# When a unit's weight blocks are split and where a side computation stands: four edits to a two-layer transformer kernel

## The chip, the cores and the metric

The kernel runs as one program on one core of a Trainium2 chip. The metric is device time in microseconds from start to end of the program. TensorE does the matmuls, VectorE (DVE) and ScalarE (ACT) the elementwise work, GpSimd (POOL) some more of it, SyncE (SP) issues most of the DMAs. Each engine runs its instructions in the order in which the program lists them.

## The reference

Two layers, each of them FFN half, mixer, FFN half, over 512 sample tokens and 128 prompt tokens (640 together) of width 1024. Every sub-layer normalises, scales and shifts its input by numbers from the condition, and adds its gated output:

```python
mod = (jax.nn.silu(cond) @ mod_w[l] + mod_b[l]).reshape(cond.shape[0], 3 * N_SUB, D_MODEL)

def adaln_sublayer(x, mod, s, g_pre, g_post, fn, weight):
    shift = mod[:, 3 * s, None]
    scale = mod[:, 3 * s + 1, None]
    gate = mod[:, 3 * s + 2, None]
    h = rmsnorm(x, g_pre) * (1 + scale) + shift
    y, aux = fn(h)
    return x + weight * gate * rmsnorm(y, g_post), aux

def swiglu(h, w_in, w_out):
    gate, up = jnp.split(h @ w_in, 2, axis=-1)
    return (jax.nn.silu(gate) * up) @ w_out
```

`w_in` is 1024 x 5632, `w_out` 2816 x 1024, and each layer has two of each. The condition has two rows (sample and prompt), so that each of the nine modulation rows of a layer is a product of a 2 x 1024 matrix with a 1024 x 1024 piece of `mod_w`. The four FFN halves hold most of the time; the change is in them.

## The kernel before

**Split products.** Every float32 factor is split in two: ScalarE casts it to the high part (`whi`, L171), VectorE subtracts that from it (`wlo`, L172), and TensorE adds three products: high with high, high with low, low with high. The weights are loaded by SP (L103) into three buffers `raw` of 512 KB, and `Stream` splits them in the order in which they are used, with at most five split blocks held.

**Parts and units.** An FFN half takes its 22 columns of 128 hidden features in six parts of 2, 4, 4, 4, 4, 4. Part 0 is done in the plain way. In parts 1 to 5 each column of 128 is a `Unit`: gate and up are one product of two by two blocks, done with seven products of blocks rather than eight. A product is 12 matmuls of 320 tokens (L717). The weight side is four blocks, X, S, Z and V. X is the gate as loaded. Four operations of GpSimd (L157, `_combine`) then make the others out of gate and up: S in a buffer of its own (`part_tile`), Z and V in the place of what was loaded. The token side is four sums of blocks of `hT`, made once per FFN half by `combine()` (L689, L692, on VectorE and GpSimd) and split into `b20` to `b41`.

**The order of a unit.** `strassen` (L790) writes it out: p2, p3 of the unit ahead, p6, p5, p7, p1 of the unit behind, p4. The products p1, p6, p7 and p4 add into one bank: between two of them ScalarE copies the bank to SBUF (L736 after p1, L747 after p6, L760 after p7), so that p7 can't begin before the copy L747 is done. Only p5 stands between. p2 ends with a subtraction on VectorE (L741) and a SiLU on ScalarE (L742), p3 with L774 on VectorE, a SiLU (L775) and a multiplication (L776); then the result is split (L379, L380) into `g`. The numbers behind the products in `strassen` say how many blocks of the next unit are split there: two after p2, one after p6, one after p4. In a part's last unit none is; there `Stream.pump` splits the blocks of `w_out` as places come free.

**Behind the units** of a part stand the products with `w_out` (L825): ten banks of 512 columns, 12 matmuls each in a part of four, evacuated by L848 or L850. In part 5 they are the tail (`emit`), with the post-norm, gate, residual and the next pre-norm.

**The side computation.** `Modulation` makes rows for later sub-layers, half a row (512 columns) at a time. `on_v` does it on VectorE: 16 operations (L438, L440), two for each of eight 128-row blocks, and then four small matmuls (L452) which sum over the partitions. `on_t` does it on TensorE with 32 matmuls (L472) in two steps. Both share three buffers `mod` of 512 KB with the accumulator. `stage` hands out the work: one half row by `on_v` beside the `w_out` products of each of parts 0 to 4, in 11 steps over that stretch (7 places in part 0, 15 in the others), the rest by `on_t` in the units of parts 1 to 4. When a stage begins, what is left of the last is issued at once. Of the 32 half rows 17 are on VectorE and 15 on TensorE.

**The last part** begins with `load_gate` (L510 to L522: the norm's weights and the two gate rows are loaded, L515 and L519, and multiplied on VectorE, L520) and `load_pre` (scale and shift for the next sub-layer, L504, with two small operations on VectorE, L507).

`in_order` pins the order of the instructions of each engine from part 0 to the end of the units.

## Time and profile before

| | |
|---|---|
| median of 2 runs | 2886.86 us (2885.67 to 2888.05) |
| the profiled execution: its own time | 2889.99 us |
| its span, first to last instruction | 2888.2 us |
| TensorE busy in it | 2595.2 us, 90% |
| mean granted TensorE clock | 0.953 |

The profile's page gives the busy time of each engine and the granted clock of TensorE in 40 slices. The waits of an engine, the order in time, and busy time and clock in chosen stretches are answers of the trace. "gap" or the number in square brackets is the idle time of the engine just before an instruction, and behind the arrow stands what ended it.

### The profile page before, as it was taken

What the parts mean: (1) busy time and instruction counts of PE and PEld (TensorE: products, weight loads), DVE (VectorE), ACT (ScalarE), POOL (GpSimd) and SP (SyncE); (2) the same over time, 40 slices, a digit from 0 to 9 for tenths busy, and PEclk for the clock granted to TensorE, in tenths of its full rate; (3) what the DMA queues carried; (4) which work ended last, traced back from release to release, by engine and by line L of the source; (5) the groups of instructions that cost most, each with busy time, mean ns of one, the idle gap of its engine ahead of it and who ended that gap; (6) DMA issues with size and microseconds to landing.
All of it is one profiled execution on the core that took longest, in us unless ns stands there. A gap on an engine that the chain in (4) does not pass through costs nothing.

```text
span 2888.2 us, 40550 instructions
## 1 busy us (share of the span) xinstructions
PE 2595.2 (90%) x15930; PEld 2295.2 (79%) x15930; DVE 1796.6 (62%) x2847; ACT 1163.5 (40%) x2179; POOL 666.4 (23%) x612
## 2 busy tenths in 40 slices
PE   7788998999989979999887899988999997999988
PEld 5677887888866868888776788877899887888877
DVE  5754566576576576665666656666777766654545
ACT  3323232464455533333253233324655653333323
POOL 1212241210010122222222222213433202222212
PEclk9899999999999989999998999999999998999999
DMA  7344454321201234443343434443222242322133
GB/s 237 96 136 126 134 174 127 117 65 52 70 25 52 97 103 119 120 127 97 82 167 88 131 120 133 119 98 117 76 64 70 63 133 61 103 74 81 52 95 110
DMA packets 356696, 296.95 MB, mean 103 GB/s; under 512 B 44364, under 2 KB 289048, under 8 KB 356504
## 3 DMA queue, kind: packets, MB, share of 16 engines
q1 hardware_dynamic: 352040, 281.25, 32.7%
q10 hardware_dynamic: 2880, 9.18, 0.8%
q0 software_dynamic: 1584, 3.93, 0.5%
q8 instruction: 125, 2.05, 0.3%
q14 instruction: 67, 0.55, 0.1%
HBM read 282.24 MB, written 15.97 MB: 103 GB/s over the span
## 4 chain that ended last, share of the span: by engine, by line
PE 41%; DVE 14%; ACT 5%; DMA 4%; issue 3%; POOL 1%; SPq 1%; ACTq 0%; DVEq 0%; POOLq 0%
PE ps L717 14%; PE ps L825 12%; DVE wlo L172 6%; PE ps L634 4%; PE ps L624 4%; ACT whi L171 4%; PE ps L1072 3%; DMA raw<-in_ffn_w_out_dram 2%; DVE mod L440 1%; PE ps L2019 1%; PE ps L2000 1%; DVE xn L689 1%; PE ps L569 1%; POOL tok L548 1%; DMA mod<-in_mod_w_dram 1%
## 5 line engine op out<-in xcount | busy, mean ns | idle before, releaser
L172 DVE TENSOR_TENSOR wlo<-raw,whi 128x1024 fp32r<-128x1024 f32 x400 | 482.8, 1225 | 245.6 <-ACT whi L171 237.5
L717 PE MATMUL ps<-hT,whi 128*128 128x320 f32 x2560 | 580.4, 314 | 0.0
L825 PE MATMUL ps<-whi,g 128*128 128x512 f32 x1760 | 572.5, 402 | 2.3 <-DVE g L380 1.1
L717 PE MATMUL ps<-b,whi 128*128 128x320 f32 x1920 | 461.1, 328 | 110.5 <-ACT tok L747 76.6
L157 POOL TENSOR_TENSOR raw<-raw 128x512 f32<-128x512 f32 x160 | 208.8, 1305 | 1410.7 <-DVE wlo L172 1157.0
L171 ACT CAST whi<-raw 128x1024 fp32r<-128x1024 f32 x400 | 409.5, 1045 | 268.8 <-PE ps L825 198.6
L717 PEld LDWEIGHTS ps<-hT,whi 128*128 128x128 f32 x2560 | 432.9, 191 | 16.0 <-issue 10.8
L717 PEld LDWEIGHTS ps<-b,whi 128*128 128x128 f32 x1920 | 344.6, 202 | 125.8 <-ACT tok L747 84.2
L717 PE MATMUL ps<-hT,wlo 128*128 128x320 f32 x1280 | 405.1, 317 | 20.3 <-DVE wlo L172 20.3
L825 PEld LDWEIGHTS ps<-whi,g 128*128 128x128 f32 x1760 | 341.1, 194 | 81.6 <-DVE g L380 3.0
L825 PE MATMUL ps<-wlo,g 128*128 128x512 f32 x880 | 353.8, 402 | 0.0
L717 PE MATMUL ps<-b,wlo 128*128 128x320 f32 x960 | 311.3, 324 | 0.0
L634 PE MATMUL ps<-hT,whi 128*128 128x384 f32 (+1 forms) x1216 | 277.9, 316 | 0.0
L717 PEld LDWEIGHTS ps<-hT,wlo 128*128 128x128 f32 x1280 | 243.6, 190 | 32.0 <-DVE wlo L172 29.7
L634 PEld LDWEIGHTS ps<-hT,whi 128*128 128x128 f32 x1216 | 204.1, 189 | 21.9 <-issue 15.2
L825 PEld LDWEIGHTS ps<-wlo,g 128*128 128x128 f32 x880 | 170.6, 194 | 37.4
L717 PEld LDWEIGHTS ps<-b,wlo 128*128 128x128 f32 x960 | 194.1, 202 | 0.0
L634 PE MATMUL ps<-hT,wlo 128*128 128x384 f32 (+1 forms) x608 | 188.8, 311 | 0.0
L440 DVE SCALAR_TENSOR_TENSOR mod<-mod,cc 128x512 f32<-128x512 f32 x238 | 183.6, 824 | 1.2 <-DMA mod<-in_mod_w_dram 1.2
L624 PE MATMUL ps<-hT,whi 128*128 128x384 f32 (+1 forms) x640 | 140.7, 311 | 1.6 <-DVE hT L380 1.6
L634 PEld LDWEIGHTS ps<-hT,wlo 128*128 128x128 f32 x608 | 114.6, 188 | 1.1 <-issue 0.8
L624 PEld LDWEIGHTS ps<-hT,whi 128*128 128x128 f32 x640 | 107.5, 190 | 2.9 <-DVE hT L380 2.5
(407 smaller groups left out, 3705.0 us busy)
## 6 DMA issues: line engine op xcount, KB each, us to landing
raw<-in_ffn_w_in_dram SPq DMA_DIRECT2D x172, 512.0 KB
mod<-in_mod_w_dram SPq DMA_DIRECT2D x128, 512.0 KB
raw<-in_ffn_w_out_dram SPq DMA_DIRECT2D x88, 512.0 KB
raw<-in_na_w_qkv_dram SPq DMA_DIRECT2D x24, 512.0 KB
raw<-in_ab_w_in_dram SPq DMA_DIRECT2D x22, 512.0 KB
raw<-in_mod_w_dram SPq DMA_DIRECT2D x32, 256.0 KB
xs<-x ACTq DMA_DIRECT2D x15, 512.0 KB
b<-xs SPq DMA_DIRECT2D x15, 512.0 KB
```

Source lines behind the costliest of these rows:

```text
L157: self.nc.gpsimd.tensor_tensor(out=out, in0=in0, in1=in1, op=op)
L171: self.nc.scalar.copy(hi[:, :k * n], raw[:, :k * n])
L172: self.nc.vector.tensor_tensor(out=lo[:, :k * n], in0=raw[:, :k * n], in1=hi[:, :k * n].bitcast(F32), op=ALU.subtract)
L440: nc.vector.scalar_tensor_tensor(out=acc[:, c], in0=raw[:, k % 2], scalar=w, in1=acc[:, c], op0=ALU.mult, op1=ALU.add)
L548: eng.tensor_tensor(out=yg[:, c0:c0 + n], in0=src, in1=G[cond_of(t)][:, c0:c0 + n], op=ALU.mult)
L569: nc.tensor.transpose(ps[k // 4][:, k % 4, :], xn[:, k * 128:(k + 1) * 128], ident)
L624: nc.tensor.matmul(out=banks[grp], lhsT=w[a][:, k, :], rhs=hT[b][:, k, o:o + n], start=(k == 0 and (a, b) == (0, 0)), stop=(k == NK - 1 an ...
L634: nc.tensor.matmul(out=banks[grp], lhsT=w[a][:, k, :], rhs=hT[b][:, k, o:o + n], start=(k == 0 and (a, b) == (0, 0)), stop=(k == NK - 1 an ...
L689: eng.tensor_tensor(out=H[key], in0=B[key][0].bitcast(F32), in1=B[key][1].bitcast(F32), op=ALU.add)
L717: nc.tensor.matmul(out=out, lhsT=w[a][:, k, :], rhs=b[c][:, k, :], start=start and (k, a, c) == (0, 0, 0), stop=(k == 3 and (a, c) == PASS ...
L825: nc.tensor.matmul(out=out, lhsT=g[a][kf][:, t * 128:(t + 1) * 128], rhs=w[b], start=(kf == 0 and (a, b) == (0, 0)), stop=(kf == len(fts) ...
L1072: nc.tensor.matmul(out=y[t][h], lhsT=hT[a][:, k, t * 128:(t + 1) * 128], rhs=ws[k // 2, h][b][:, k % 2, :], start=(k == 0 and (a, b) == (0 ...
```

## The change

1. **Splits.** One block after each of p2, p7, p1 and p4 of a unit that isn't the last of its part, rather than two after p2 and one each after p6 and p4; the unit's first p2 takes part too. What p2 does on ScalarE (SiLU) is issued after the block's split. What p3 does on ScalarE, and the multiplication, waits until p6 of the next unit has issued its copy (`rest` in `Unit.later`).
2. **Modulation.** None in part 0. One half row on VectorE in each of parts 1 to 4, one step after each p5 and five beside the `w_out` products; its loads are 256 KB each, in two buffers `mraw`, the accumulator is `macc`. Half rows on TensorE are spread evenly over parts 1 to 4, with the buffers `G1` and `traw`. Now 14 half rows are on VectorE and 18 on TensorE.
3. **S** lies in two halves of one buffer, `G0`, or `macc` in the last part, rather than in `G0` and `G1` by turns.
4. **Gates.** In the last part the norm's weights and the two gate rows are loaded one by one after p7 of its first three units, and multiplied where the scheduler finds a place.

`qkn` moved from one pool to another, and the scratch `junk` to another buffer.

```diff
 class Modulation:
+        def __init__(self, pool, todo, n_v):
+            units = [(l, r, h) for l, r in todo for h in range(D // self.N)]
+            n_t = max(len(units) - n_v, 0)
+            self.loads = {
+                "v": [(*u, k, 1) for u in units[n_t:] for k in range(NK)],
+                "t": [(*u, k, 2) for u in units[:n_t] for k in range(0, NK, 2)],
+            }
...
+        def load(self, kind):
+            while self.loads[kind] and len(self.raws[kind]) < 2:
+                l, r, h, k, n = self.loads[kind].pop(0)
+                if kind == "v":
+                    raw = self.pool.tile([128, 1, self.N], F32, tag="mraw", name="mraw", bufs=2)
+                elif next(self.turn) % 2:
+                    raw = self.pool.tile([128, 2, self.N], F32, tag="traw", name="traw", bufs=1)
+                else:
+                    raw = state.tile([128, 2, self.N], F32, tag="G1", name="G1")
+                nc.sync.dma_start(out=raw, in_=kblock(I["mod_w"][l], k, n, r * D + h * self.N, self.N))
...
+        def start(self, places):
+
+            self.load("v")
+            self.load("t")
+            self.rate, self.owed = 3 * self.n_t / places, 0.0
+
+        def tick(self, v=False):
+            if v:
+                next(self.v, None)
             self.owed += self.rate
             while self.owed >= 1.0:
                 self.owed -= 1.0
-                next(self.it, None)
+                next(self.t, None)
...
-    def load_gate(l, s, weight):
+    def gate_steps(l, s, weight):
 
         gp = big("tok", [128, D])
         nc.sync.dma_start(out=gp, in_=I["norm_post"][l, s].partition_broadcast(128))
+        yield
         out = []
         for c in range(2):
             g = state.tile([128, D], F32, tag=f"G{c}", name=f"G{c}")
             nc.sync.dma_start(out=g, in_=modrows[l][3 * s + 2][c].partition_broadcast(128))
+            out.append(g)
+            yield
+        for g in out:
             nc.vector.scalar_tensor_tensor(out=g, in0=g, scalar=weight, in1=gp, op0=ALU.mult, op1=ALU.mult)
-            out.append(g)
-        return out
+        yield out
...
             def p2(self):
                 W, t = bank([128, HALF]), self.t
                 self.product(W, self.half(self.X, 1), B[1, 0], True)
                 nc.vector.tensor_tensor(out=t[:, 0], in0=t[:, 0], in1=W, op=ALU.add)
-                nc.scalar.activation(out=t[:, 0], in_=t[:, 0], func=AF.Silu)
                 self.done("X")
+                return lambda: nc.scalar.activation(out=t[:, 0], in_=t[:, 0], func=AF.Silu)
...
                 nc.vector.tensor_tensor(out=t[:, 1], in0=t[:, 1], in1=self.Z, op=ALU.add)
-                nc.scalar.activation(out=t[:, 1], in_=t[:, 1], func=AF.Silu)
-                nc.vector.tensor_tensor(out=t[:, 1], in0=t[:, 1], in1=t[:, 2], op=ALU.mult)
+
+                def rest():
+                    nc.scalar.activation(out=t[:, 1], in_=t[:, 1], func=AF.Silu)
+                    nc.vector.tensor_tensor(out=t[:, 1], in0=t[:, 1], in1=t[:, 2], op=ALU.mult)
+                    self.out(1 if self.last else 0, 2)
...
-                todo = [(u.p1, ())] if begin else []
-                todo.append((u.p2, () if begin else (item, item)))
+                todo = [(u.p1, 0)] if begin else []
+                todo.append((u.p2, 1))
                 if not begin:
-                    todo.append((us[i - 1].p3, ()))
-                todo += [(u.p6, () if end else (item,)), (u.p5, ()), (u.p7, ())]
-                todo.append((fill if end else us[i + 1].p1, ()))
-                todo.append((u.p4, () if end else (item,)))
+                    todo.append((us[i - 1].p3, 0))
+                todo += [(u.p6, 0), (u.p5, 0), (u.p7, 1), (fill if end else us[i + 1].p1, 1), (u.p4, 1)]
...
+                    after = fn()
...
+                    for _ in range(0 if end else n):
+                        item()
+                    if after:
+                        after()
                     stream.pump()
+                    if fn == u.p7 and gates and not end:
+                        next(gates)
+                    tick(fn == u.p5)
...
-                mod.stage("t", len(mod.units), 1)
-                mod.stage("t", 0, 1)
-                stream.part_tile = lambda: fp.tile([128, 512], F32, tag="mod", name="mod", bufs=3)
-                G = load_gate(l, s, 0.5)
+                mod.finish()
+                stream.part_tile = part_tiles(lambda: fp.tile([128, 2, 512], F32, tag="macc", name="macc", bufs=1))
+                gates = gate_steps(l, s, 0.5)
...
-                if not last:
-                    mod.stage("t", n_t[p], 7 * len(fts))
-                strassen(fts, g, fill)
+                if p == 1:
+                    mod.start(sum(11 * n - 1 for n in PARTS[1:-1]))
+                strassen(fts, g, fill, gates if last else None)
...
-                mod.stage("v", 1, 4 * len(fts) - 1)
-                for _ in outs:
+                for n, _ in enumerate(outs):
                     stream.pump()
-                    tick()
+                    tick(p > 0 and n in (2, 4, 6, 8, 12))
```

ScalarE in the first FFN half, part 1, from the third unit's p4 to the last unit's p7. `whi` is the high part of a block, `ps` a bank, `tok` and `xn` hold a unit's three products. Before (`raw_1073`, `raw_1217` are the last unit's gate and up, `raw_1223` and `raw_1388` the first two blocks of `w_out`):

```order
L171 CAST whi_1365<-G1_1285 128x512
L742 ACTIVATE tok_1337<-tok_1337 128x320
L171 CAST whi_1384<-raw_1217 128x1024
L171 CAST whi_1390<-raw_1073 128x1024
L171 CAST whi_1396<-raw_1223 128x1024
L775 ACTIVATE xn_1166<-xn_1166 128x320
L171 CAST whi_1422<-raw_1388 128x1024
L747 COPY tok_1337<-ps_1338 128x320
L379 CAST g0_2_905<-xn_1166 128x640
L171 CAST whi_1443<-raw_1394 128x1024
L760 COPY tok_1337<-ps_1338 128x320
```

Now (`raw_1005`, `raw_1141` are the last unit's gate and up, `raw_1160` and `raw_1289` the first two blocks of `w_out`):

```order
L171 CAST whi_1266<-G0_1025 128x512
L759 COPY tok_1270<-ps_1271 128x320
L171 CAST whi_1285<-raw_1141 128x1024
L171 CAST whi_1304<-raw_1005 128x1024
L171 CAST whi_1324<-raw_1160 128x1024
L766 ACTIVATE tok_1270<-tok_1270 128x320
L171 CAST whi_1349<-raw_1289 128x1024
L770 COPY tok_1270<-ps_1271 128x320
L800 ACTIVATE xn_1122<-xn_1122 128x320
L387 CAST g0_2_861<-xn_1122 128x640
L171 CAST whi_1372<-raw_1308 128x1024
L783 COPY tok_1270<-ps_1271 128x320
```

The SiLU of p3 (L775, now L800) went from ahead of the copy after p6 (L747, now L770) to behind it. The cast of the second block of `w_out` stands ahead of that copy in both; the last unit's Z and V, whose splits free the buffers into which that block and the one after it are loaded, went from behind p2 to behind p1 and p4.

VectorE in the first FFN half at the end of part 0, where the token side's blocks are made and split. Before:

```order
L172 TENSOR_TENSOR wlo_846<-raw_684,whi_845 128x1024
L692 TENSOR_TENSOR xn_749<-xn_749,tok_747 128x1280
L440 SCALAR_TENSOR_TENSOR mod_770<-mod_804,cc_93,mod_770 128x512 x2
L380 TENSOR_TENSOR b21_717<-xn_749,b20_716 128x1280
L440 SCALAR_TENSOR_TENSOR mod_770<-mod_804,cc_93,mod_770 128x512 x2
L380 TENSOR_TENSOR b31_719<-xn_748,b30_718 128x1280
L692 TENSOR_TENSOR tok_750<-tok_750,xn_749 128x1280
L380 TENSOR_TENSOR b41_721<-tok_750,b40_720 128x1280
L455 TENSOR_TENSOR mrow_765<-ps_891,mrow_765 128x256
L741 TENSOR_TENSOR xn_911<-xn_911,ps_926 128x320
```

Now:

```order
L172 TENSOR_TENSOR wlo_818<-raw_684,whi_817 128x1024
L715 TENSOR_TENSOR xn_745<-xn_745,tok_743 128x1280
L388 TENSOR_TENSOR b21_717<-xn_745,b20_716 128x1280
L388 TENSOR_TENSOR b31_719<-xn_744,b30_718 128x1280
L715 TENSOR_TENSOR tok_746<-tok_746,xn_745 128x1280
L388 TENSOR_TENSOR b41_721<-tok_746,b40_720 128x1280
L764 TENSOR_TENSOR xn_875<-xn_875,ps_890 128x320
L172 TENSOR_TENSOR wlo_905<-raw_696,whi_904 128x1024
L455 TENSOR_SCALAR macc_939<-mraw_867,cc_93 128x512 x2
L784 TENSOR_TENSOR xn_875<-xn_875,ps_926 128x320
```

The half row's 16 operations are gone from between the token side's, and the first step of one now stands in the first unit of part 1.

VectorE in the first FFN half at the start of the last part, up to the second unit's p7. `mcol` holds scale and shift for the next sub-layer. Before:

```order
L850 TENSOR_TENSOR x4_715<-x4_715,ps_4100 128x512
L455 TENSOR_TENSOR mrow_3981<-ps_4141,mrow_3981 128x256
L520 SCALAR_TENSOR_TENSOR G0_4153<-G0_4153,tok_4151 128x1024
L520 SCALAR_TENSOR_TENSOR G1_4156<-G1_4156,tok_4151 128x1024
L507 SCALAR_TENSOR_TENSOR mcol_4159<-mcol_4159,gcol_4160 128x8 x2
L741 TENSOR_TENSOR xn_4168<-xn_4168,ps_4183 128x320
```

Now (`...` stands for the rest of the first unit):

```order
L878 TENSOR_TENSOR x4_715<-x4_715,ps_4135 128x512
L527 SCALAR_TENSOR_TENSOR mcol_4186<-mcol_4186,gcol_4187 128x8 x2
L764 TENSOR_TENSOR xn_4195<-xn_4195,ps_4210 128x320
...
L764 TENSOR_TENSOR tok_4280<-tok_4280,ps_4320 128x320
L172 TENSOR_TENSOR wlo_4335<-raw_4152,whi_4334 128x1024
L797 TENSOR_TENSOR xn_4195<-xn_4195,ps_4247 128x320
L801 TENSOR_TENSOR xn_4195<-xn_4195 128x320
L388 TENSOR_TENSOR g1_0_4182<-xn_4195,g0_0_4178 128x640
L544 SCALAR_TENSOR_TENSOR G0_4404<-G0_4404,tok_4278 128x1024
```

The gate rows' multiplications (L520, now L544) stood ahead of the first unit's L741; now the first of them stands in the second unit, behind its p6. The two operations on `mcol` stay where they were.

## Rows read from the trace of the kernel before

**Rows 1.** The page: busy time of the engines, and TensorE's granted clock in 40 slices of the span.

```profile
PE 2595.2 (90%) x15930; PEld 2295.2 (79%) x15930; DVE 1796.6 (62%) x2847; ACT 1163.5 (40%) x2179; POOL 666.4 (23%) x612
...
PEclk9899999999999989999998999999999998999999
```

**Rows 2.** The waits of TensorE: what waited for what, microseconds in total, how many times, the longest.

```profile
PE ps L717 <- ACT tok L747: 76.6, 29, 4.2
PE ps L452 <- DVE mod L440: 63.0, 4, 16.1
PE ps L717 <- ACT xn L747: 33.9, 13, 8.8
PE ps L472 <- DMA mod<-in_mod_w_dram: 27.5, 10, 7.0
PE ps L717 <- DVE wlo L172: 20.3, 36, 0.7
```

**Rows 3.** The order in time, TensorE: the product p7 that waits for L747 in the last unit of a part, the first and the last of 20; then the same in the first unit of an FFN half's last part, the first and the last of 4. Columns: start, microseconds, engine, line, operation, names, shapes, count, and in brackets the idle time before and what ended it.

```profile
171.50 0.90 PE L717 MATMUL ps<-b,whi 128*128 128x320 f32 x2 [3.88 <-ACT tok L747]
...
2844.87 0.90 PE L717 MATMUL ps<-b,whi 128*128 128x320 f32 x2 [3.46 <-ACT tok L747]
...
506.85 0.90 PE L717 MATMUL ps<-b,whi 128*128 128x320 f32 x2 [7.40 <-ACT xn L747]
...
2798.13 0.90 PE L717 MATMUL ps<-b,whi 128*128 128x320 f32 x2 [5.62 <-ACT xn L747]
```

**Rows 4.** The order in time around one of the 20, in the second FFN half, engine by engine: TensorE, ScalarE, SyncE.

```profile
1092.48 0.64 PE L717 MATMUL ps<-b,whi 128*128 128x320 f32 x2 [4.00 <-ACT tok L747]
...
1091.06 1.04 ACT L171 CAST whi<-raw 128x1024 fp32r<-128x1024 f32 x1 [1.00 <-DMA raw<-in_ffn_w_out_dram]
1092.01 0.42 ACT L747 COPY tok<-ps 128x320 f32<-128x320 f32 x1
...
1086.72 2.63 SPq L103 DMA_DIRECT2D raw<-in_ffn_w_out_dram  x3
```

**Rows 5.** The chain of work that ended last, in order of time: two products L717 of a unit, back to back, and the products L825 behind them.

```profile
1098.13 3.52 PE ps L717 x24
1101.65 25.78 PE ps L825 x111
```

**Rows 6.** Stretches of time: length, busy time of PE, PEld, DVE, ACT, POOL with counts, granted clock, DMA share, GB/s. The first is behind the wait of rows 4, the second the bubble at the end of a part 0, the third behind a wait at the start of a last part.

```profile
1092.40:1098.10 5.70, 5.62 (x22) 5.18 (x23) 3.41 (x4) 2.13 (x4) 0.00 (x0) 0.70 0.65 209
1021.60:1037.60 16.00, 0.00 (x0) 0.00 (x0) 16.00 (x18) 6.11 (x8) 0.00 (x0) 0.59 0.58 164
1407.20:1414.00 6.80, 6.79 (x37) 6.80 (x38) 1.71 (x2) 2.27 (x4) 4.49 (x4) 0.77 0.01 2
```

**Rows 7.** The order in time at the end of part 0 of the second FFN half: TensorE's next work, and p7 of the first unit; VectorE's first sum of the token side and its last split; GpSimd's two sums.

```profile
1037.65 1.64 PE L452 MATMUL ps<-mod,ones 128*32 128x256 f32 x8 [16.08 <-DVE mod L440]
...
1047.43 0.46 PE L717 MATMUL ps<-b,whi 128*128 128x320 f32 x2
...
1009.79 4.24 DVE L689 TENSOR_TENSOR xn<-hT,hT 128x1280 f32<-128x1280 f32 x1
1018.05 1.48 DVE L689 TENSOR_TENSOR xn<-hT,hT 128x1280 f32<-128x1280 f32 x1
...
1042.30 1.49 DVE L380 TENSOR_TENSOR b<-tok,b 128x1280 fp32r<-128x1280 f32 x1 [1.33 <-ACT b L379]
...
1009.15 7.70 POOL L689 TENSOR_TENSOR tok<-hT,hT 128x1280 f32<-128x1280 f32 x2
```

**Rows 8.** The same stretch, busy time of the lines L440 and L438 alone: length, busy time of DVE with count, granted clock, DMA share, GB/s.

```profile
1009.70:1043.80 34.10, 9.66 (x14) 0.75 0.27 77
1009.70:1043.80 34.10, 3.57 (x2) 0.75 0.27 77
```

**Rows 9.** The order in time at the start of the same FFN half's last part: TensorE's p1 and p7 of the first unit, SyncE, VectorE.

```profile
1393.33 0.56 PE L717 MATMUL ps<-hT,whi 128*128 128x320 f32 x2
...
1407.20 0.90 PE L717 MATMUL ps<-b,whi 128*128 128x320 f32 x2 [6.58 <-ACT xn L747]
...
1395.67 0.36 SPq L515 DMA_DIRECT2D tok<-in_norm_post_dram  x1
...
1397.50 4.92 SPq L504 DMA_DIRECT2D mcol<-mod  x2
...
1405.77 0.17 DVE L507 SCALAR_TENSOR_TENSOR mcol<-mcol,gcol 128x8 f32<-128x8 f32 x1 [1.26 <-DMA mcol<-mod]
```

**Rows 10.** The order in time, TensorE: one modulation step that doesn't wait.

```profile
1068.61 1.08 PE L472 MATMUL ps<-mod,cc 128*32 128x128 f32 x32
```

**Rows 11.** Groups of instructions by line and shape: busy time, mean ns of one, idle time before.

```profile
L172 DVE TENSOR_TENSOR wlo<-raw,whi 128x1024 fp32r<-128x1024 f32 x400 | 482.8, 1225 | 245.6 <-ACT whi L171 237.5 <-issue 1.2 <-PE ps L1295 0.7
...
L157 POOL TENSOR_TENSOR raw<-raw 128x512 f32<-128x512 f32 x160 | 208.8, 1305 | 1410.7 <-DVE wlo L172 1157.0 <-DMA mrow<-in_mod_b_dram 69.3 <-DMA raw<-in_ffn_w_in_dram 42.1
```

**Rows 12.** The order in time, VectorE: two modulation operations and a split of S with GpSimd idle, then the same beside GpSimd's operations.

```profile
1390.41 1.40 DVE L440 SCALAR_TENSOR_TENSOR mod<-mod,cc 128x512 f32<-128x512 f32 x2
...
1379.06 0.68 DVE L172 TENSOR_TENSOR wlo<-G,whi 128x512 fp32r<-128x512 f32 x1
...
1376.20 2.94 DVE L440 SCALAR_TENSOR_TENSOR mod<-mod,cc 128x512 f32<-128x512 f32 x2
...
1081.79 1.80 DVE L172 TENSOR_TENSOR wlo<-G,whi 128x512 fp32r<-128x512 f32 x1
```

More of the change, by code (lines that the diff above doesn't have):

```diff
@@ L421, in bias @@
+        def bias(self, l, r, h, n, parts):
+            tag = f"mrow{n}"
+            row = self.pool.tile([128, n], F32, tag=tag, name=tag, bufs=1)
+            c0 = r * D + h * self.N
             for p, o in parts:
@@ L467, in on_t @@
                 for i in range(2):
-                    raw = self.raws.pop(0)
+                    raw = self.raws["t"].pop(0)
                     for k2 in range(2):
@@ L475, in on_t @@
                             )
-                self.load()
+                self.load("t")
+                if q == 0:
+                    row = self.bias(l, r, h, n, parts)
                 yield
```

122 lines of the change are left out of this document (54 added, 68 removed).

## The prediction

> **What bounds the kernel now.** I read the page first: TensorE is busy for 90% of the span, at a mean clock of 0.953 [rows 1]. So about 290 us are idle, and more is lost to the lower clock; nothing but TensorE's own waits is worth a look. Next its waits [rows 2]. Five of them make 221 us, and all lie in the four FFN halves, in places that the change touches. Then the order in time at each place:
>
> *Ends of parts.* In each part's last unit p7 waits for the copy L747, 20 times, at most 4.2 us [rows 2, 3]. Added up one by one they are 73 of the 76.6 us on `tok`, 3.7 us each. ScalarE is held by the cast of a `w_out` block that is still under way: its load was issued at 1086.72, as soon as the last unit's Z was split, and p7 began at 1092.48, 5.8 us later [rows 4].
>
> *Ends of part 0.* Four waits of 16 us for the modulation's accumulator [rows 2, 7]. VectorE does the half row between the operations that make the token side.
>
> *Starts of last parts.* Four waits of 5.6 to 8.8 us [rows 2, 3], with 28 of the 33.9 us on `xn`. VectorE stands at the gate rows' and `mcol`'s loads, p2's subtraction behind them [rows 9].
>
> *Modulation on TensorE* waits 27.5 us for its loads, and there are 29 us of short waits: 20.3 for `wlo`, the rest for L747 [rows 2].
>
> Behind a long wait the granted clock is 0.70 over 5.7 us, and 0.77 over 6.8 us [rows 6]: parts at 1.2 GHz instead of 2.4. TensorE had stood idle just before. That costs 0.30 x 5.7 = 1.7 us and 0.23 x 6.8 = 1.6 us more. At full clock a product takes 3.52 / 2 = 1.76 us [rows 5], a unit of seven 12.3 us.
>
> **The change, part by part.** *Splits.* The last unit's Z is now split behind its p1, with p4, p2, p3, p6 and p5 before p7: 5 x 1.76 = 8.8 us. Cast 1.05 and subtraction 1.23 [rows 4, 11] and the copy of p1 ahead of them (0.42 as L747) end 2.7 us after p1, and the 5.8 us from the load's issue to p7 are then over at 8.5 us. So the wait would just go. But where a modulation step now stands beside the unit, VectorE is later. GpSimd's four operations, 1.3 us each [rows 11], run in the same stretch, and beside them two modulation operations took 2.94 us, not 1.40, and a split of S 1.80, not 0.68 [rows 12]. I count 1.5 us of lateness, with 0 and 4 us (the wait of today) as the bounds, in the 14 parts that have such a step, and 0.3 in the other 6. That leaves 23 of 73 us: **50 us gained**. Of the slow clock, 20 x 1.7 = 34 us, I take two thirds: **23**.
>
> The short waits for `wlo` and L747 should nearly all go. Z is split three products earlier, and p3's SiLU no longer stands ahead of the copy that p7 needs. I leave 5 of 29: **24**.
>
> Taking the splits forward asks for the loads sooner. From the end of p1 to p6 of the next unit, which needs S, stand ten products, 17.6 us. Z's split (up to 4.6 us with the lateness above), two GpSimd operations (2.6), S's cast (half a block's, 0.6 as estimated from 1.04 for a whole one) and its split (1.8) take 9.6, so a load may take 8 us before TensorE feels it. One took 4.3 in the rows: the cast of 1091.06 waited for it from 1086.72 [rows 4]. What remains is load traffic of the modulation beside it; I charge **10 us** for new waits in the units, bounds 0 and 60.
>
> *Part 0.* VectorE loses 9.66 + 3.57 = 13.2 us of modulation in that stretch [rows 8]. Its last split ended at 1042.30 + 1.49 = 1043.8, so now at 1030.6. On the other side the second sum L689 (1.48 us alone) moves up beside GpSimd's 7.70 us and will take 4.2 as the first does [rows 7]: 1033.3. Then p2's subtraction, SiLU and the copy follow, 0.5 each by the copy's row [rows 4], and p7 begins at about 1034.9 instead of 1047.43. That is 12.5 us four times, slow clock included: **50**. TensorE still stands some 6 us there, since p1 could start at 1021.6 and p7 at 1028.6.
>
> *Last part.* The gate loads leave SyncE's queue ahead of `mcol`'s: 1395.67 to 1397.50 [rows 9]. The last half row on VectorE ends three of 15 places sooner, which is 24 of 120 matmuls of 25.78 / 111 = 0.23 us [rows 5], or 5.5 us, so that SyncE is past its store earlier too. Both bring `mcol`'s last operation, 1405.77, to about 1398.7, before p7 is due at 1393.3 + 4 x 1.76 = 1400.4 less the 1.5 us of subtraction, SiLU and copy. The multiplications now stand behind p6 of the second and third unit, and there VectorE may wait a little for a gate row; S and Z of the next unit have over 3 us in hand. I leave 3 of 28: **25**, and **6** for the clock. On SyncE the two gate rows are now queued ahead of `w_out` loads; at 0.4 us an issue that is hidden as long as those have the 8 us above.
>
> *Modulation on TensorE.* Even spacing over 172 places puts a step with its two loads at every seventh place or later, and a unit of 12.3 us has seven; three loads issued within 2.63 us began to land after 4.3 [rows 4], so two should be there in time. I leave 2 of 27.5: **25**, and **5** for the clock, bounds 0 and 10. Three more half rows cost 6 steps of 1.1 to 1.3 us [rows 10], 7 us; three groups L452 fewer give back 2: **minus 5**.
>
> *VectorE in all.* 48 operations fewer but more of them beside GpSimd. With a modulation step a unit asks VectorE for three splits of 1.23, one of 1.8, the two operations of 2.9, and some 3.3 us of small ones, 11.7 us of a unit's 12.3. That fits, with little to spare. About this the Trainium skill ("SBUF — State Buffer", section "SBUF: two separate sides") says that VectorE with two SBUF inputs and GpSimd take one shared port pair as an exclusive lock, the loser waiting for a whole instruction. By that rule the 2.94 us would be usual, and GpSimd late as well. The trace agrees as far as 2.94 against 1.40 goes [rows 12].
>
> **Sum.** 50 + 23 + 24 - 10 + 50 + 25 + 6 + 25 + 5 - 5 = 193 us. The profiled execution's own time is 2889.99, 3 us above the median of 2886.86: 2890 - 193 = 2697, and against the median 2694. I predict **2695 us**, 6.7% less.
>
> **Rivals.** *All of it goes.* The waits are 221 us and the clock behind them about 34 + 6 + 8; less the 5 us of added work and part 0's unavoidable 24 that is 240: 2650 us. For it speaks that the 8.5 us just fit into 8.8. Chance 0.2.
>
> *VectorE becomes the bound in the units.* 56 units carry a modulation step. If operations beside GpSimd cost as in rows 12 and GpSimd is held up in turn, each unit is 1 us longer, 56 us, and the ends of parts keep two thirds of their wait, 25 us more, with the clock 10: 2785 us. Against it speaks the 11.7 of 12.3. By the skill's rule this is the way it goes; the rule counts in this chance, 0.2.
>
> *SyncE's one queue makes it slower.* Its order now mixes weight loads with 256 KB loads that wait for VectorE and 512 KB loads that wait for TensorE. A weight load behind one of them is as late as it is. It decides once a load needs over 8 us from its place in the queue to landing. To lose 2% it would take 193 + 58 = 251 us, or 4.2 us in each of the 60 units that aren't a part's first (4 x 5 x 3), so a load of 12 us. Rows 4 have three issues in 2.63 us and nothing near that: 2945 us, chance 0.05.
>
> *It does not do what it says:* p7's copy is held by the `w_out` cast as before, since the load is still issued too late, and part 0 is held by its own sums. Then only the modulation's waits and the last part's gain stays, some 60 us: 2830 us, chance 0.07.
>
> **Chances and range.** The forecast, 2660 to 2740, has 0.48. The range should take in the first two rivals: 2640 to 2790. A measurement of this kernel can tell about 2% from no change. Faster by over 2% means under 2829: 0.48 + 0.2 + 0.2 and half of the last rival, 0.91. Slower 0.05, the same 0.04.
>
> **What would show it.** Right: the waits of p7 for the copy behind p6 fall from 110 us to under 40; none of 16 us behind part 0, with 5 to 8 us instead; none above 2 us at the start of a last part; L472 waits for next to nothing; the granted clock is above 0.97. Wrong: new waits of p5, p6 or p7 for `wlo` or a SiLU in units with a modulation step (VectorE), casts on ScalarE that wait for weights loaded by SyncE in the middle of a part (the queue), or a bubble behind part 0 as long as before.

## The result and the profile after

The changed kernel takes **2651.26 us** (median of 2 runs, 2650.78 to 2651.73) against 2886.86: ratio 0.918, 95% interval 0.914 to 0.922. That is 236 us less, where the forecast's sum was 193 us and its range reached from 2640 to 2790.

From the page after, for [rows 1]:

```profile
PE 2528.0 (95%) x16098; PEld 2250.9 (85%) x16098; DVE 1821.9 (69%) x2797; ACT 1170.8 (44%) x2179; POOL 718.0 (27%) x612
...
PEclk9899999999999999999999999999999999999999
```

TensorE does 168 matmuls more and is busy 67 us less; the difference to the span, its idle time, fell from 293 to 121 us. So 172 us of the gain are waits and 67 are matmuls that run sooner at the higher clock (mean 0.984 instead of 0.953). TensorE's waits after, in the places of [rows 2], in microseconds, times and the longest:

```profile
PE ps L740 <- ACT xn L759: 34.1, 4, 8.9
...
PE ps L740 <- ACT tok L770: 8.6, 10, 1.6
...
PE ps L740 <- ACT xn L770: 2.7, 3, 1.4
PE ps L740 <- DVE tok L784: 2.4, 8, 0.6
...
PE ps L740 <- ACT tok L783: 1.2, 2, 0.6
```

L740 is the product (before L717), L770 the copy behind p6 (before L747), L759 the copy of p1. No wait for `wlo`, for modulation loads or for the modulation's accumulator is left. The new wait is that of p6 for the copy of p1 behind part 0, 8.87 to 8.88 us three times and once 7.52. The 8.6 us for L770 on `tok` stand at ten of the 20 ends of parts.

The place of [rows 4] after the change: TensorE's p7, ScalarE and SyncE.

```profile
1002.58 0.56 PE L740 MATMUL ps<-b,whi 128*128 128x320 f32 x2
...
1001.15 1.05 ACT L171 CAST whi<-raw 128x1024 fp32r<-128x1024 f32 x1 [1.33 <-DMA raw<-in_ffn_w_out_dram]
1002.11 0.41 ACT L770 COPY tok<-ps 128x320 f32<-128x320 f32 x1
...
997.42 3.43 SPq L103 DMA_DIRECT2D raw<-in_ffn_w_out_dram  x3
```

The cast of the `w_out` block still waits for its load and still stands ahead of the copy. But the load left 5.2 us before p7 was due, where it was 1.8 us before (1092.48 less the wait of 4.00 and 1086.72 in [rows 4]), and p7 shows no wait. In the ten ends that are left the load is still the last thing that ScalarE waits for: it waits 1.4 to 2.7 us for it at the cast, and the copy stands behind. The longest of them, ScalarE and TensorE:

```profile
396.11 1.04 ACT L171 CAST whi<-raw 128x1024 fp32r<-128x1024 f32 x1 [1.60 <-DMA raw<-in_ffn_w_out_dram]
397.06 0.42 ACT L770 COPY tok<-ps 128x320 f32<-128x320 f32 x1
...
397.53 0.57 PE L740 MATMUL ps<-b,whi 128*128 128x320 f32 x2 [1.59 <-ACT tok L770]
```

What the clock gave back shows in the units of a whole part: the third one with units in the second FFN half, before and then after, columns as in [rows 6]:

```profile
1216.20:1277.90 61.70, 57.10 (x412) 54.79 (x409) 31.02 (x41) 24.34 (x39) 15.28 (x12) 0.94 0.42 129
```

```profile
1119.00:1172.80 53.80, 53.80 (x410) 52.28 (x409) 38.56 (x47) 24.63 (x39) 17.52 (x12) 1.00 0.47 142
```

The same 410 or so matmuls take 7.9 us less: 4.6 us of waits and 3.3 of TensorE's own time at a clock of 1.00 instead of 0.94. VectorE now does 38.6 us there instead of 31.0, beside more of GpSimd (17.5 instead of 15.3), and TensorE doesn't wait for it.

### The profile page after: what moved, and what is told of

It is laid out like the page before. It is cut to its first block, busy times and chain, and to the rows that moved or that the text cites. A ratio compares the mean times of both kernels' runs of the same rounds, so it can differ in the third digit from the quotient of the medians.

```text
span 2649.0 us, 40880 instructions
## 1 busy us (share of the span) xinstructions
PE 2528.0 (95%) x16098; PEld 2250.9 (85%) x16098; DVE 1821.9 (69%) x2797; ACT 1170.8 (44%) x2179; POOL 718.0 (27%) x612
## 4 chain that ended last, share of the span: by engine, by line
PE 50%; DVE 8%; DMA 3%; issue 2%; ACT 2%; POOL 1%; SPq 0%; DVEq 0%; POOLq 0%; ACTq 0%
PE ps L740 21%; PE ps L853 13%; PE ps L660 5%; PE ps L650 4%; PE ps L1101 3%; DVE wlo L172 2%; DMA raw<-in_ffn_w_out_dram 2%; ACT whi L171 1%; DVE macc L457 1%; DMA G<-mod 1%; PE ps L2048 1%; PE ps L2029 1%; PE ps L484 1%; POOL tok L574 1%; PE ps L595 1%
## 5 line engine op out<-in xcount | busy, mean ns | idle before, releaser
L740 PE MATMUL ps<-hT,whi 128*128 128x320 f32 x2560 | 570.8, 311 | 2.4 <-DVE tok L784 2.4
L171 ACT CAST whi<-raw 128x1024 fp32r<-128x1024 f32 x400 | 418.4, 1051 | 348.6 <-PE ps L853 204.8
L157 POOL TENSOR_TENSOR raw<-raw 128x512 f32<-128x512 f32 x160 | 232.6, 1454 | 1131.4 <-DVE wlo L172 688.2
L740 PE MATMUL ps<-b,whi 128*128 128x320 f32 x1920 | 435.2, 314 | 46.7 <-ACT xn L759 34.1
L740 PEld LDWEIGHTS ps<-hT,whi 128*128 128x128 f32 x2560 | 430.3, 189 | 9.1 <-DVE tok L784 4.5
L740 PE MATMUL ps<-hT,wlo 128*128 128x320 f32 x1280 | 396.7, 310 | 0.0
L740 PEld LDWEIGHTS ps<-b,whi 128*128 128x128 f32 x1920 | 324.2, 190 | 57.8 <-ACT xn L759 35.2
L740 PE MATMUL ps<-b,wlo 128*128 128x320 f32 x960 | 298.9, 311 | 0.0
L740 PEld LDWEIGHTS ps<-hT,wlo 128*128 128x128 f32 x1280 | 241.5, 189 | 0.0
L660 PEld LDWEIGHTS ps<-hT,whi 128*128 128x128 f32 x1216 | 204.1, 189 | 21.9 <-issue 15.2
L457 DVE SCALAR_TENSOR_TENSOR macc<-mraw,cc,macc 128x512 f32<-128x512 f32 x196 | 209.7, 1115 | 0.0
L740 PEld LDWEIGHTS ps<-b,wlo 128*128 128x128 f32 x960 | 182.5, 190 | 0.0
L878 DVE TENSOR_TENSOR x<-x,ps 128x512 f32<-128x512 f32 x160 | 106.2, 684 | 24.6 <-PE ps L853 22.7
```

Source lines behind the costliest of these rows:

```text
L157: self.nc.gpsimd.tensor_tensor(out=out, in0=in0, in1=in1, op=op)
L171: self.nc.scalar.copy(hi[:, :k * n], raw[:, :k * n])
L457: nc.vector.scalar_tensor_tensor(out=acc[:, c], in0=raw[:, 0], scalar=w, in1=acc[:, c], op0=ALU.mult, op1=ALU.add)
L660: nc.tensor.matmul(out=banks[grp], lhsT=w[a][:, k, :], rhs=hT[b][:, k, o:o + n], start=(k == 0 and (a, b) == (0, 0)), stop=(k == NK - 1 an ...
L740: nc.tensor.matmul(out=out, lhsT=w[a][:, k, :], rhs=b[c][:, k, :], start=start and (k, a, c) == (0, 0, 0), stop=(k == 3 and (a, c) == PASS ...
L878: nc.vector.tensor_tensor(out=dst, in0=dst, in1=acc[t], op=ALU.add)
```

## Experiments

Each ratio is against the kernel before, run on the same chip; differences to the change are the difference of the ratios times 2886.86 us.

### One half of the unit's order undone, the other, and both

Old places for the splits:

```diff
-                todo.append((u.p2, 1))
+                todo.append((u.p2, 0 if begin else 2))
-                todo += [(u.p6, 0), (u.p5, 0), (u.p7, 1), (fill if end else us[i + 1].p1, 1), (u.p4, 1)]
+                todo += [(u.p6, 1), (u.p5, 0), (u.p7, 0), (fill if end else us[i + 1].p1, 0), (u.p4, 1)]
-                    for _ in range(0 if end else n):
+                    for _ in range(0 if end and fn != u.p2 else n):
```

> The changed kernel with one thing undone: a unit's blocks are split where they were before (two behind p2, one behind p6, one behind p4, and in the last unit two behind p2), so the last unit's Z is split behind its p2 and the w_out load leaves from there. The later SiLU order stays. Theory (the earlier split gives the load and cast of w_out their time, and most of the gain at the ends of parts comes from that alone): p7's 20 waits for the copy come back at about 3.7 us each, 74 us, with some 1.7 us each of slow clock, 34, and a few short waits: 80 to 110 us above the change, 2730 to 2760. Rival (p3's SiLU ahead of the copy held it, and the split places do little): at most 20 us above, under 2672.

Measured: 2726.41 us, ratio 0.946 (0.944 to 0.948), 79 us above the change. Its waits:

```profile
PE ps L740 <- ACT tok L770: 42.9, 20, 2.4
...
PE ps L740 <- DVE wlo L172: 21.8, 36, 0.7
```

The rival falls: the places are worth 79 us. But p7's 20 waits come back at 2.1 us each, not at 3.7, and all 36 waits for `wlo` with them. In each of the 20, the cast ahead of the copy waited 2.3 to 3.8 us for its `w_out` load, as here:

```profile
1109.58 1.04 ACT L171 CAST whi<-raw 128x1024 fp32r<-128x1024 f32 x1 [2.45 <-DMA raw<-in_ffn_w_out_dram]
```

Old SiLU order:

```diff
+                nc.scalar.activation(out=t[:, 0], in_=t[:, 0], func=AF.Silu)
                 self.done("X")
-                return lambda: nc.scalar.activation(out=t[:, 0], in_=t[:, 0], func=AF.Silu)
...
+                nc.scalar.activation(out=t[:, 1], in_=t[:, 1], func=AF.Silu)
+                nc.vector.tensor_tensor(out=t[:, 1], in0=t[:, 1], in1=t[:, 2], op=ALU.mult)
                 def rest():
-                    nc.scalar.activation(out=t[:, 1], in_=t[:, 1], func=AF.Silu)
-                    nc.vector.tensor_tensor(out=t[:, 1], in0=t[:, 1], in1=t[:, 2], op=ALU.mult)
                     self.out(1 if self.last else 0, 2)
```

> The changed kernel with p2's SiLU put back ahead of the next pump of loads and p3's SiLU and multiplication put back behind p3, so only the split of the product stays deferred to p6. Splits stay at their new places. Theory (the SiLU order is worth the short waits only): 5 to 30 us above the change, 2656 to 2680, as waits of 0.3 to 0.6 us a unit for the copy behind p6. Rival (the order on ScalarE is what lets the copy through at the ends of parts): 80 us or more above, over 2730.

Measured: 2710.66 us, ratio 0.940 (0.938 to 0.941), 62 us above: both expectations missed, and the order is worth much more than the short waits. At the end of a part, ScalarE and TensorE in the order in time:

```profile
1103.82 0.47 ACT L798 ACTIVATE xn<-xn 128x320 f32<-128x320 f32 x1 [1.69 <-DVE xn L797]
1104.19 1.03 ACT L171 CAST whi<-raw 128x1024 fp32r<-128x1024 f32 x1
1105.13 0.42 ACT L770 COPY tok<-ps 128x320 f32<-128x320 f32 x1
...
1105.60 0.76 PE L740 MATMUL ps<-b,whi 128*128 128x320 f32 x2 [2.11 <-ACT tok L770]
```

The SiLU of p3 waits 1.69 us for VectorE, at the head of ScalarE's queue, and the `w_out` cast and the copy stand behind it. The split alone is early; the copy is late all the same. The waits for this copy are 57.3 us in all, 41 of them, where the change has 11.3, 13 of them; 38 of the 41 have p3's SiLU ahead of the copy, the other three (5.3 us) p2's.

Both undone, which leaves the modulation's places and buffers and the gate loads:

> The changed kernel with both undone, the split places and the SiLU order: what is left of the change is the modulation's new places and buffers and the gate loads one by one. Undone alone they cost 75 us (old places) and 59 us (old SiLU order). Theory (the copy is held by a sum of latenesses, the cast of w_out and p3's SiLU, each of which the other one's cure partly hides): both together cost about 180 us as in the kernel before, 2820 to 2845, since the splits and the SiLU order alone took 179 us off the kernel before. Rival (they add up): 134 us, 2775 to 2795.

Measured: 2799.03 us, ratio 0.971 (0.969 to 0.972), 151 us above the change; the two apart come to 141. So they nearly add up, though the time lies just above the rival's range, and the rest of the change alone takes 85 us off the kernel before. The 20 waits of p7 at the ends of parts show the same sum: 8.6 us in the change, 42.9 with the old places, 36.2 with the old SiLU order, 68.2 with both. p7's copy is the old wait again:

```profile
PE ps L740 <- ACT tok L770: 75.0, 37, 4.1
...
PE ps L740 <- DVE wlo L172: 24.8, 39, 0.7
```

### The unit's order alone, on the kernel before

The same lines as in the two diffs above, the other way round, put into the kernel before.

> The kernel before with the split places and the SiLU order of the change and nothing else of it: modulation in its old places and buffers, gate loads at once. Theory: the ends of parts (73 us and about 34 of slow clock) and the short waits (29) go, while part 0's 63 us, the last parts' 28 and the modulation's own 27 stay, as does the VectorE's load: 110 to 140 us below before, 2747 to 2777. Rival (splits alone are undone by the half rows that VectorE still does at the ends of parts): 50 to 90 below, 2797 to 2837.

Measured: 2704.54 us, ratio 0.938 (0.936 to 0.940): 179 us below the kernel before, three quarters of the whole gain, and above what either theory allowed.

```profile
PE ps L452 <- DVE mod L440: 63.0, 4, 16.1
PE ps L717 <- ACT xn L747: 27.6, 4, 8.2
...
PE ps L472 <- DMA mod<-in_mod_w_dram: 12.9, 10, 2.9
```

Not one of the 20 waits at the ends of parts is left, nor one for `wlo`; the 63 us behind part 0 stand unchanged, and the modulation's waits have halved without any edit to it. With the 85 us of the other parts that makes 264 for a change that gives 236, so 28 us are counted in both.

### The half row in part 0

```diff
-        mod = Modulation(fp, todo, len(PARTS) - 2)
+        mod = Modulation(fp, todo, len(PARTS) - 1)
...
+                if p == 0:
+                    mod.load("v")
                 for n, _ in enumerate(outs):
                     stream.pump()
-                    tick(p > 0 and n in (2, 4, 6, 8, 12))
+                    tick(p == 0 or n in (2, 4, 6, 8, 12))
+                if p == 0:
+                    tick(True)
```

> The changed kernel with a fifth half row of the modulation on VectorE, beside part 0's w_out products, as the kernel before had it there, and one half row fewer on TensorE. Theory (VectorE's 13 us of half row held the end of part 0, and their removal gave 29 us of waits and some clock): the four waits behind part 0 grow by 8 to 12 us each, less 2 us of TensorE work each: 30 to 45 us above the change, 2680 to 2697. Rival (part 0's end is set by the token side's sums and ScalarE's queue, and the row finds room beside them): 0 to 10 us above.

Measured: 2691.98 us, ratio 0.933 (0.932 to 0.935), 43 us above. TensorE waits for that row again, 20 us each time, in place of the 34.1 us for the copy of p1:

```profile
PE ps L466 <- DVE macc L457: 80.2, 4, 20.4
```

### The gate loads first

```diff
-                gates = gate_steps(l, s, 0.5)
+                G = load_gate(l, s, 0.5)
-                strassen(fts, g, fill, gates if last else None)
+                strassen(fts, g, fill)
-        G = next(gates)
```

> The changed kernel with the gate rows loaded and multiplied all at once ahead of the last part, as before, and not one by one behind its units. Theory (the gate loads ahead of mcol's on SyncE's queue are what made p7 of the last part's first unit wait): four waits of 5 to 8 us come back, with some slow clock: 25 to 35 us above the change, 2676 to 2686. Rival (the half row that now ends earlier on VectorE and SyncE is enough by itself): within 8 us of it, 2643 to 2659.

Measured: 2674.09 us, ratio 0.926 (0.925 to 0.928), 23 us above. The theory holds, a little under its bound: the four waits are back with 26.2 us. VectorE in the order in time, at the start of the first FFN half's last part:

```profile
440.33 2.41 DVE L544 SCALAR_TENSOR_TENSOR G<-G,tok 128x1024 f32<-128x1024 f32 x2 [8.11 <-DMA G<-mod]
...
443.20 0.17 DVE L527 SCALAR_TENSOR_TENSOR mcol<-mcol,gcol 128x8 f32<-128x8 f32 x1 [0.46 <-DMA mcol<-mod]
444.52 0.17 DVE L527 SCALAR_TENSOR_TENSOR mcol<-mcol,gcol 128x8 f32<-128x8 f32 x1 [1.16 <-DMA mcol<-mod]
444.61 0.48 DVE L764 TENSOR_TENSOR xn<-xn,ps 128x320 f32<-128x320 f32 x1
```

VectorE idles 8.11 us at the gate rows; `mcol`'s operations and p2's subtraction, the last line, are behind them. The edit moves the gate rows' multiplications on VectorE together with their loads, but the loads alone would do: when the multiplications are over, `mcol`'s own loads, queued behind the gate rows', are still awaited (0.46 and 1.16 us).

### Spacing or buffers of the modulation's loads

```diff
-                    mod.start(sum(11 * n - 1 for n in PARTS[1:-1]))
+                    mod.start(sum(7 * n + 1 for n in PARTS[1:-1]))
...
-                    tick(p > 0 and n in (2, 4, 6, 8, 12))
+                    tick(p > 0 and n in (2, 4, 6, 8, 12), False)
```

(with the second argument False, `tick` makes no step on TensorE)

> The changed kernel with TensorE's modulation steps spread over the units' places only, 116 places and not 172, and none beside the w_out products, so that the steps come half again as close, as in the kernel before. Theory (the spacing over all places took the 27 us of waits for its loads away): 10 to 25 us above the change, 2661 to 2676. Rival (its own two buffers did, since a load leaves as soon as its own step has read the buffer): within 6 us of it.

Measured: 2651.54 us, ratio 0.918 (0.917 to 0.920), no difference. The waits for those loads are 5.8 us in all, against 27.5 in [rows 2]:

```profile
PE ps L484 <- DMA traw<-in_mod_w_dram: 3.1, 4, 0.8
PE ps L484 <- DMA G<-in_mod_w_dram: 2.7, 4, 1.2
```

So the spacing isn't what cured it. The modulation's own buffers, and the unit's order, which alone had halved the waits, are what remains as causes; they weren't tried apart.

### VectorE's half rows away from the units

```diff
-                    tick(fn == u.p5)
+                    tick()
...
-                    tick(p > 0 and n in (2, 4, 6, 8, 12))
+                    tick(p > 0 and n in (1, 2, 3, 4, 5, 6, 8, 10, 12))
```

> The changed kernel with all nine steps of a VectorE half row beside the w_out products, none in the units behind p5. Theory (in the kernel before with only the splits and the SiLU order, no p7 waited, while in the changed one 13 waits of 0.2 to 1.6 us are left, 11 us in all: they come from the half row's steps in the units, beside GpSimd's four operations a unit): those waits go: 10 to 20 us below the change, 2631 to 2641. Rival (VectorE is not tight, the waits come from loads or elsewhere, or wait for the products' sums instead): within 6 us of it.

Measured: 2681.71 us, ratio 0.930 (0.929 to 0.932), 34 us **slower** than the change: the theory was half right. p7 waits twice, 0.5 and 0.4 us. But TensorE now waits for the rows' end (first line), and VectorE waited for the rows' own loads (second line; a group with its mean ns and the idle time before it):

```profile
PE ps L466 <- DVE macc L457: 32.6, 14, 6.6
```

```profile
L457 DVE SCALAR_TENSOR_TENSOR macc<-mraw,cc,macc 128x512 f32<-128x512 f32 x196 | 156.6, 849 | 28.4 <-DMA mraw<-in_mod_w_dram 27.6
```

Eight of the nine steps ask for a 256 KB load each, from two buffers, and so close together faster than they come. Part by part, these late loads can account for at most 25 of the 32.6 us. In 12 of the 14 parts TensorE's wait is longer than they were late; what made the rest isn't shown. The same group in the changed kernel:

```profile
L457 DVE SCALAR_TENSOR_TENSOR macc<-mraw,cc,macc 128x512 f32<-128x512 f32 x196 | 209.7, 1115 | 0.0
```

There an operation costs a third more in the mean (1115 ns against 849), since four of a row's nine steps stand in the units, and no load is late.

### What is left behind part 0

```diff
-                lambda: (whole_of(b12, nc.vector), whole_of(b11, nc.gpsimd)),
-                lambda: whole_of(b22, nc.vector),
-                lambda: (minus(b11, b12, b11), whole_of(b21, nc.gpsimd)),
+                lambda: (whole_of(b12, nc.vector), whole_of(b11, nc.vector)),
+                lambda: (whole_of(b22, nc.vector), minus(b11, b12, b11)),
...
-                lambda: (split(H[b12], *C[3]), minus(b21, b21, b22)),
+                lambda: split(H[b12], *C[3]),
+                lambda: (whole_of(b21, nc.vector), minus(b21, b21, b22)),
```

> The changed kernel with the token side's eight sums and differences behind part 0 all on VectorE, none on GpSimd, in an order that gives C1 first. Theory (the 8.5 us that p6 still waits behind part 0, four times, come from VectorE's sums and splits beside GpSimd, 7.7 us each, and from the casts that stand ahead of p1's copy on ScalarE): the four waits of 34 us fall to about 8, with a little slow clock back: 20 to 40 us below the change, 2611 to 2631. Rival (ScalarE's casts still wait for the same VectorE chain, which is now longer by two sums): within 8 us of it.

Measured: 2638.61 us, ratio 0.915 (0.914 to 0.916), 10 us below: half the expectation. The sums are done sooner, but the four waits only fell from 34.1 to 29.1 us, because the copy of p1 still stands behind the cast for the last split, and that waits for VectorE. In the next run that last split (C4) is one place later; its sum and its difference are two entries of the list instead of one:

```diff
-                lambda: (whole_of(b21, nc.vector), minus(b21, b21, b22)),
+                lambda: whole_of(b21, nc.vector),
+                lambda: minus(b21, b21, b22),
```

> The kernel with the token side's sums all on VectorE, and the last of its four splits one place later, behind p1 of the first unit, so that ScalarE copies p1 before it casts for that split. Theory (in that run p6 waited 29 us for the copy of p1, which stood behind the cast of the last split, and that cast waited for VectorE, while p6 itself needs only the split that was done 4 to 5 us sooner): the four waits go, to under 5 us, and some slow clock: 20 to 35 us below the run with the sums on VectorE, about 2605 to 2618. Rival (p6 or p7 then waits for its own operand's split, or p4 for the last): under 8 us gained.

Measured: 2629.03 us, ratio 0.912 (0.910 to 0.913), 9 us below that run: neither expectation. The waits fell to 13.0 us. ScalarE's copy of p1 is no longer behind the cast; it now waits for its buffer, which the third split still reads:

```profile
947.90 0.42 ACT L760 COPY xn<-ps 128x320 f32<-128x320 f32 x1 [0.64 <-DVE b L388]
```

The third split (C3) later too, and the half rows beside `w_out` with their last step at the end:

```diff
-                lambda: split(H[b12], *C[3]),
...
+                lambda: None,
+                lambda: split(H[b12], *C[3]),
...
-                    tick(fn == u.p5)
+                    tick()
...
-                    tick(p > 0 and n in (2, 4, 6, 8, 12))
+                    tick(p > 0 and n in (1, 2, 4, 5, 6, 8, 9, 10, 14))
```

(b22 also takes its buffer ahead of b12)

> The run with the last token-side split one place later, and two more edits: the third split too behind p1 (C3, with C4 behind p2), so that no cast stands ahead of p1's copy on ScalarE; and the nine steps of a VectorE half row beside the w_out products as in the run that had them there, but the last, which TensorE waited for, two places later, at the end of them. Theory: of the 13 us that p6 still waited for p1's copy about 10 go, and of the 17 us behind p6 and p7 about 12, while TensorE waits little for the row's end (before, 33 us at the earlier place): 18 to 28 us below that run, 2601 to 2611. Rival (the row's end is still awaited, 1 us or more a part, or p7 waits for C3): 2620 to 2645.

Measured: 2644.91 us, ratio 0.916 (0.915 to 0.917), 13 us above the run before it; the rival holds. 15.4 us of waits for the rows' end are new, and the copy is as late as it was, since its buffer is now read by the last difference, L715:

```profile
955.75 0.43 ACT L761 COPY xn<-ps 128x320 f32<-128x320 f32 x1 [2.13 <-DVE tok L715]
```

So a last version takes both out: the units' two buffers in the other order, and the row's last step behind p5 of the next part's first unit (behind part 4, it is issued ahead of the last part; b12 takes its buffer first again):

```diff
-                self.t = big(("tok", "xn")[Unit.count % 2], [128, 4, HALF])
+                self.t = big(("xn", "tok")[Unit.count % 2], [128, 4, HALF])
...
-                    tick()
+                    tick(begin and p > 1 and not last and fn == u.p5)
...
-                    tick(p > 0 and n in (1, 2, 4, 5, 6, 8, 9, 10, 14))
+                    tick(p > 0 and n in (1, 2, 4, 5, 6, 8, 9, 10))
```

> The run with the last token-side split one place later, with three more edits. C3's split is behind p1 and C4's behind p2. The units take their two tiles in the other order, so that p1's copy writes to the buffer that C1's split left long ago: in the run before, that copy was late because its buffer was still read by the last difference, and in the one before that by C3's split. And eight steps of a VectorE half row stand beside the w_out products, at the places of that run, while the ninth, for whose matmul TensorE waited 15 us, stands behind p5 of the next part's first unit. Theory: p6's 13 us of waiting for p1's copy fall to about 7 (the copy is then only behind the five copies of the products), the 17 us behind p6 and p7 to about 6, and the row's end costs under 3: 14 to 22 us below that run, 2608 to 2617. Rival (the waits move once more, to C3 for p7 or to the row's end): within 8 us of it, 2621 to 2637.

Measured: **2616.92 us**, ratio 0.907 (0.906 to 0.908): 33 us below the change and the fastest here, at the edge of what the theory gave.

```profile
PE ps L742 <- ACT tok L772: 13.4, 7, 2.8
PE ps L742 <- ACT tok L761: 5.9, 3, 2.0
...
PE ps L466 <- DVE macc L457: 1.5, 1, 1.5
```

p6's waits are 5.9 us now, and the row's end costs 1.5. What is left for the copy behind p6 (L772) didn't go as expected: 2.5 to 2.8 us in the first unit of three last parts, and 1.5 to 1.7 behind three of the parts 0.

## Why the prediction was right, and where it was off

Sign, places and range were right, and every sign named for "right" is there but one: 8.9 us behind part 0, not 5 to 8. The sum was 43 us short. By its terms, against what the trace after shows:

| term | forecast | measured |
|---|---|---|
| waits at the ends of parts | 50 | 64 (73 to 8.6) |
| short waits, less new ones in the units | 24 - 10 | 25 (29 to 3.6, all that is left or new) |
| waits at the starts of last parts | 25 | 25 (28 to 2.7) |
| the modulation's loads | 25 | 27.5 |
| part 0, clock included | 50 | 32 |
| slow clock elsewhere | 23 + 6 + 5 | some 70 (below) |

**The slow clock is the term that was furthest off.** "Of the slow clock, 20 x 1.7 = 34 us, I take two thirds: 23" rests on one row, 0.70 over 5.7 us [rows 6]. Others of the 20 in the kernel before show the spread; these are the first 5.7 us behind three more of the same waits:

```profile
1180.00:1185.70 5.70, 5.62 (x19) 5.21 (x20) 3.31 (x4) 2.12 (x4) 0.00 (x0) 0.56 0.57 182
1267.97:1273.67 5.70, 5.62 (x18) 5.14 (x19) 3.40 (x4) 2.12 (x4) 0.00 (x0) 0.50 0.60 196
...
1452.84:1458.54 5.70, 5.62 (x35) 5.35 (x36) 3.71 (x5) 2.13 (x4) 0.00 (x0) 1.00 0.74 230
```

Over all 20 the mean is 0.63, so 20 x 0.37 x 5.7 = 42 us. After the change the clock over the units is 1.00 in all parts but part 1 (0.92 there, with the wait for the copy of p1 in it), so about all of it came back. The 6 us for the last parts stand on the highest of four rows, too: 0.77 [rows 6], where the other three have 0.58, 0.70 and 0.65 over as long, which makes 9 us. The 5 us for the clock behind the modulation's waits were too little as well: in the four parts that have one of over 5 us, the granted clock over the units was 0.88 to 0.91, and 0.94 to 0.97 in the rest but the last parts. TensorE's busy time says the same from the other side: 67 us less, with some 5 us of added work by the forecast's count, so 72 given back, 3 of them in the row of part 0.

**Part 0 was overrated.** From the end of the `w_out` products (946.6) to the first unit's p7 it is now 17.8 us, before 25.8 [rows 6, 7]: 8.0 us four times, 32, not 50. "p7 begins at about 1034.9" counted VectorE's work and one operation late beside GpSimd's sums. That one came: a split of S at 3.45 us, rather than the second sum, which took 1.48. But VectorE now waits twice for ScalarE's cast between a sum and its split, 1.32 us each, where modulation stood in one of these places before ([rows 7] have one such wait, 1.33). So its last split ends 25.3 us after its first sum begins, not 23.5. VectorE and GpSimd:

```profile
934.80 4.24 DVE L712 TENSOR_TENSOR xn<-hT,hT 128x1280 f32<-128x1280 f32 x1
938.97 3.45 DVE L172 TENSOR_TENSOR wlo<-G,whi 128x512 fp32r<-128x512 f32 x1
942.34 1.48 DVE L712 TENSOR_TENSOR xn<-hT,hT 128x1280 f32<-128x1280 f32 x1
...
953.02 2.89 DVE L388 TENSOR_TENSOR b<-xn,b 128x1280 fp32r<-128x1280 f32 x2 [1.32 <-ACT b L387]
...
958.64 1.49 DVE L388 TENSOR_TENSOR b<-tok,b 128x1280 fp32r<-128x1280 f32 x1 [1.32 <-ACT b L387]
...
934.16 7.71 POOL L712 TENSOR_TENSOR tok<-hT,hT 128x1280 f32<-128x1280 f32 x2
```

And the copy of p1 stands on ScalarE behind the casts for the last splits, so it is p6 that waits, not p7, and p6 and p5 still have to run. p7 (the last line) begins 4.3 us behind VectorE's last split, not 1.6:

```profile
957.35 1.26 ACT L387 CAST b<-tok 128x1280 fp32r<-128x1280 f32 x1 [2.23 <-DVE tok L715]
958.52 0.42 ACT L759 COPY xn<-ps 128x320 f32<-128x320 f32 x1
...
958.99 0.90 PE L740 MATMUL ps<-b,whi 128*128 128x320 f32 x2 [8.87 <-ACT xn L759]
...
964.44 0.46 PE L740 MATMUL ps<-b,whi 128*128 128x320 f32 x2
```

The runs under "What is left behind part 0" bear that out: p6's waits fell from 34.1 to 5.9 us as the sums left GpSimd and then this queue and a buffer were cleared; 4.9 of that came back at p7.

**Ends of parts.** Mechanism right, lateness overrated (23 us left by the forecast, 8.6 in the trace). Where a wait is left, it is of the kind that the forecast named, a load that still comes too late. What the text gave to the split alone is two causes: the places of the splits, with the load of `w_out` that hangs on them (79 us, with the waits for `wlo` and the clock), and p3's SiLU at the head of ScalarE's queue (62 us, put back together with p2's). The prediction named the second for the short waits only. It also put 87 us on the unit's order (50 + 23 + 24 - 10), which alone gives 179, and 106 on the rest, which alone gives 85.

**The modulation on TensorE.** Right in size, wrong in its reason: the even spacing was given the credit, and without it nothing changes.

**The rivals.** The time is that of "all of it goes" (2650), but not by its terms: it left 24 us behind part 0, where 34 are left, and counted 48 us of clock, where 70 came back. VectorE did not become the bound. Its work in the units is as dense as feared, and TensorE's idle time over the stretch of 53.80 us above is nil. The rule of the Trainium skill that went into this rival ("SBUF — State Buffer", section "SBUF: two separate sides": VectorE with two SBUF inputs and GpSimd lock each other out for a whole instruction) agrees with the longer operations (1115 ns with four steps of nine in the units, 849 with none, 3.45 us for a split that takes 0.68 alone in [rows 12]). What it costs is decided by who waits for the late operation, and in the units nobody did for long. Of the third rival's loads on SyncE's queue, those of `w_out` are behind the ten waits that are left at the ends of parts, 8.6 us in all; no engine waits for the modulation's weights in the changed kernel, and where eight of a row's came close together, their lateness was behind most of the waits in a run that lost 34 us.

## What to carry to other kernels

An in-order engine that copies for the critical product holds it up through whatever stands ahead in its queue: go through the queue entry by entry (a cast that waits for a load, a SiLU that waits for another engine), since clearing one leaves the next. Here the two were worth 79 and 62 us, each with what moved along with it. A wait costs TensorE more than its length; take the clock behind it from all its occurrences, not from one row. And a buffer's old readers are a queue too: twice the copy moved ahead in its engine's order and was then held by the buffer it writes to.

## Not expected of the hardware

The same wait of some 4 us is followed by a granted clock of anything between 0.50 and 1.00 over the next 5.7 us: nine of 20 at 0.50 to 0.56, ten at 0.70 to 0.74, one at 1.00. A short wait left it alone: over the 14.3 us around one of 0.65 for `wlo` it was 1.00.

```profile
1250.00:1264.30 14.30, 13.65 (x92) 13.12 (x90) 8.48 (x10) 6.98 (x11) 5.09 (x4) 1.00 0.46 146
```
